# Step sizes as plain fp32 products of 64 columns, packed first loads, and gate weights stored in two pieces

## The chip, the cores and the metric

The kernel runs on one core of one Trainium2 chip. The metric is device time in microseconds (us). The kernel before takes 1026.54 us, the median of three runs (1025.41 to 1026.98). One more execution was taken by the hardware profiler: 1022.72 us, of which the span from the first to the last instruction is 1020.9 us. Every reading of the trace below is of that execution.

The core has a matmul engine (PE, with its weight loads listed apart as PEld), a vector engine (DVE), a scalar engine (ACT), a general engine (POOL) and the queue that issues most transfers (SP). Each takes its own instructions in order; they meet through semaphores.

## The reference

The program computes two decoder layers over one sequence of 256 tokens of width 2048: a Mamba-2 layer (layer A), then sliding-window attention (layer B). What this change touches, cut from the reference:

```python
# layer A
zxbcdt = x @ w_in                       # z 4096, xs 4096, B 1024, C 1024, dt 64 columns
dt = softplus(dt_raw + dt_bias)         # 256 x 64: the step sizes, one for each head
a  = -exp(a_log)
da_cum = cumsum(dt * a)                 # within a chunk of 128
decay  = exp(segsum(dt * a))            # scales every head's C B^T
# layer B
proj = x @ w_in                         # [q 2048 | gate 2048]
o = attention(q, k, v) * silu(gate)
```

All 64 step sizes are needed before any head's decay can be formed, and so before the first group of heads can finish.

## The kernel before

A product of full precision is made of three matmuls of the type fp32r (helper `mac`): each operand is split in a high part (ACT copies it to fp32r) and a low part (DVE subtracts that copy from the raw value), and high times high, high times low and low times high are summed in PSUM. The operand that is loaded into the array is a tile of weights (`wh`, `wl`), the one that streams is 256 tokens of x (`xH`, `xL`) or, in layer B, of the first layer's output (`x1H`, `x1L`).

Weights come in units of 128 columns by 2048 rows, 1 MB each, in the order of the list `srcs`. A unit is fetched by two transfers on SP into raw tiles (`wr`, five buffers), split on ACT and DVE (`load_unit`, L106 to L120), and multiplied in 16 tiles of 128 rows times three matmuls, 48 in all (`gemm_ws`, L273). `next_unit` (L170) keeps two units ahead of the one in use. Layer A has eight groups of ten units; group 0 begins with its four z units, then B, C and four xs units. The program's order inside each engine is fixed when the program is built, by a scheduler with costs and priorities of its own.

The start is special (`load_first`, L122, and L537): the first two units are the one of the step sizes (`wdt`, whose 64 columns are laid down twice to fill 128) and the first z unit. They are fetched beside x in six pieces of two to four tiles, and their matmuls alternate by pieces. The block of the step sizes then goes to `make_dt` (L290): ACT adds the bias, a chain of some twenty small operations on DVE makes the softplus and the running sums, the result goes to HBM (`rscr`, L318), and `load_decay` (L357) fetches rows of it, copied to all partitions, into `rb`. `sum_decay` (L369) makes the exponents of four heads from it, `cb` (L415) and `ymm` (L447) use them. The chain's DVE operations stand between the splits of the next units.

Where x stands in memory matters to the matmuls' pace. The class `Split` (L218) puts the first two tiles of `xH` and `xL` at bytes 0 and 64 modulo 256 and the rest at 192, while layer A's weights begin at 0. In layer B, `x1H` and `x1L` begin at 0. The 16 gate units of layer B (`gate_block`, L761: four blocks for each of j = 0 to 3) are shifted as a whole by 16 elements, 64 bytes (`split_tiles(16)`, L99 and L181), and so have their weights at 64.

Two more places of the program are named below: `ymm` multiplies plain fp32 tiles of 64 columns, two at a time, which write to rows 0 to 63 and 64 to 127 of one PSUM tile (L459); `cb` multiplies plain fp32 tiles of 128 columns (L419, L420).

Of the kernel before, what the change touches and what calls it, by code (L numbers as in the profile page):

```python
# [15 lines left out]
P = 128  # L16
S = 256
# [40 lines left out]
def trunk(ctx: ExitStack, tc: tile.TileContext, A: dict, out: bass.AP, dbg=None):  # L58
# [17 lines left out]
    def nm(s):  # L76
        uid[0] += 1
        return f"{s}_{uid[0]}"
# [15 lines left out]
    nc.gpsimd.memset(eps_t[:], EPS)  # L94

    class Unit:
        __slots__ = ("h", "l")

    def split_tiles(at):  # L99

        return [
            wp.tile([P, 2112], F32R, tag=tag, name=nm(tag), bufs=n)[:, at : at + 2048]
            for tag, n in (("wh", NH), ("wl", NL))
        ]

    def load_unit(src, at=0):  # L106
        u = Unit()
        hi, lo = split_tiles(at)
        raws = []
        for c in range(2):  # L110
            raw = wp.tile([P, 1024], F32, tag="wr", name=nm("wr"), bufs=NR)
            nc.sync.dma_start(raw[:], src[:, c * 1024 : (c + 1) * 1024])
            raws.append(raw)
        for c in range(2):
            sl = slice(c * 1024, (c + 1) * 1024)
            nc.scalar.activation(hi[:, sl], raws[c][:], AF.Copy)  # L116
            nc.vector.tensor_tensor(lo[:, sl], raws[c][:], hi[:, sl].bitcast(F32), ALU.subtract)  # L117
        u.h = hi
        u.l = lo
        return u  # L120

    def load_first(ss):  # L122

        us = [Unit() for _ in ss]
        for u in us:
            u.h, u.l = split_tiles(0)
        xraws = [
            ap.tile([P, 6, S], F32, tag="e", name=nm("xraw"), bufs=2),
            ap.tile([P, 6, S], F32, tag="e", name=nm("xraw"), bufs=2),
            ap.tile([P, 4, S], F32, tag="yz", name=nm("xraw"), bufs=1),  # L130
        ]
        for k0, k1 in FIRST:
            n = k1 - k0
            sl = slice(k0 * P, k1 * P)
            xraw = xraws[k0 // 6][:, k0 % 6 : k0 % 6 + n, :]
            for i, u in enumerate(us):
                raw = wp.tile([P, 1024], F32, tag="wr", name=nm("wr"), bufs=NR)[:, : n * P]
                nc.sync.dma_start(raw, ss[i][:, sl])
                if i == 0:
                    nc.sync.dma_start(xraw, A["xt"][:, k0:k1, :])  # L140
                nc.scalar.activation(u.h[:, sl], raw, AF.Copy)
                nc.vector.tensor_tensor(u.l[:, sl], raw, u.h[:, sl].bitcast(F32), ALU.subtract)
                if i == 0:
                    nc.scalar.activation(xH(k0, k1), xraw, AF.Copy)  # L144
                    nc.vector.tensor_tensor(xL(k0, k1), xraw, xH(k0, k1).bitcast(F32), ALU.subtract)  # L145
        return us


    srcs = [A["wdt"]]

    def wo_srcs(name, j):
        return [A[name][j * 4 + i] for i in range(4)]
# [9 lines left out]
    shifted = set()  # L162
    for what, j in B_ORDER:
        if what == "g":
            shifted.update(range(len(srcs), len(srcs) + 4))
        srcs += wo_srcs({"q": "wq", "g": "wg", "o": "wb"}[what], j)
    units = []
    used = [0]

    def next_unit():  # L170
        if not units:
            units.extend(load_first(srcs[:NFIRST]))
            nc.sync.dma_start(pc[:], A["pc"])
        while len(units) < min(used[0] + 1 + AHEAD, len(srcs)):
            if len(units) == 5:
                nc.sync.dma_start(cc[:], A["cc"])
            if len(units) in (8, 9):
                i = len(units) - 8
                nc.sync.dma_start(xr[:, i, :], A["xk"][:, i, :])
                nc.scalar.activation(xr[:, i, :], xr[:, i, :], AF.Copy, scale=ALPHA)  # L180
            units.append(load_unit(srcs[len(units)], 16 if len(units) in shifted else 0))  # L181
        used[0] += 1
        return units[used[0] - 1]

# [85 lines left out]
            stats(1, nb)  # L270
        done(1)

    def gemm_ws(us):  # L273
        pss = [mm_tile() for _ in us]
        for k0, k1 in FIRST:
            for ps, u in zip(pss, us):
                for k in range(k0, k1):
                    ks = slice(k * P, (k + 1) * P)
                    mac(
                        ps[:, :S], u.h[:, ks], u.l[:, ks], xH(k, k + 1)[:, 0, :], xL(k, k + 1)[:, 0, :],  # L280
                        k == 0, k == KT - 1,
                    )
        return pss


# [4 lines left out]
    def make_dt(ps):  # L290
        f = [ap.tile([P, S], F32, tag="sm", name=nm("f"), bufs=NSM) for _ in range(7)]
        u, e, rec, z, w, q, dt = [x[:] for x in f]
        nc.scalar.activation(u, ps[:, :S], AF.Identity, bias=pc[:, PC_DTB : PC_DTB + 1])
# [210 lines left out]

    def group(g):
        for b in range(10):
            if g == 0 and b < NFIRST - 1:
                ps = first_ps[b + 1]
            else:
                ps = gemm_ws([next_unit()])[0]  # L510
            k = BLOCKS0[b] if g == 0 else BLOCKS[b]
            if k >= 6:
                in_z(g, k - 6, ps)
            elif k >= 2:
                in_xs(g, k - 2, ps)
            else:
                (in_b, in_c)[k](g, ps)
            for fn, *a in plan.pop(10 * g + b, ()):
                fn(*a)
            if b in OUT_AT[g]:  # L520
                out_units(g - 1, [OUT_AT[g].index(b)])
        if g == NG - 1:
            out_units(g - 1, [1])
            out_units(g - 1, [2, 3])
            for t in sorted(plan):
                for fn, *a in plan[t]:
                    fn(*a)
        elif g > 0:
            out_units(g - 1, range(len(OUT_AT[g]), 4))
# [4 lines left out]
            for h in range(2):  # L534
                out_unit(*gs[g].y, h, u, nb, False, gs[g].rms)

    first_ps = gemm_ws([next_unit() for _ in range(NFIRST)])  # L537

    for c0, c1 in ((PC_CONV, PC_CONV + 240), (PC_NW, PC_NW + 32)):
        nc.vector.tensor_scalar(pc[:, c0:c1], pc[:, c0:c1], 0.5, None, ALU.mult)  # L540

    with tc.high_priority():
        dts = make_dt(first_ps[0])
        load_decay(0, 0)


    cs = cst.tile([P, 2, 8], F32, tag="cs", name="cs")
# [213 lines left out]
    def gate_block(j):  # L761
        t = bp.tile([P, 4, S], F32, tag="sg", name=nm("sg"), bufs=2)
        sg[j] = t
        for p_ in range(4):
            u = next_unit()
            ps = mm_tile()
            for k in range(KT):
                ks = slice(k * P, (k + 1) * P)
# [154 lines left out]
def _layout(inputs):  # L923
# [29 lines left out]
    a["wdt"] = wstat(np.concatenate([w[:, o_dt:], w[:, o_dt:]], 1))[0]  # L953
    conv = np.concatenate([f["a_conv_w"][0], f["a_conv_b"]], 0)
    corder = []
    for g in range(NG):
# [53 lines left out]
```

## Time and profile before

| | |
|---|---|
| median of three runs | 1026.54 us |
| profiled execution | 1022.72 us |
| its span, first to last instruction | 1020.9 us |
| PE busy | 1004.8 us, 98% of the span |
| DVE, ACT, POOL busy | 804.4, 519.5, 84.9 us |
| granted PE clock, mean | 0.999 of full speed |
| bytes read from HBM | 200.13 MB |

PE is busy nearly everywhere, and so a stage is worth reading at two places: where PE stands idle or works slowly (the start, single waits, the end), and at the step from the start of one matmul to the start of the next. The listed duration of a matmul (280 ns) is longer than that step, because matmuls overlap in the array. A plain fp32 matmul shows as two records in the trace. A row of the timeline has the start and the duration in us, the engine, the line of the kernel, the operation, the tiles (output, then inputs), the shapes and the count; a bracket has the idle time before it and what ended it.

### The profile page before, as it was taken

The numbers are of one execution on the slowest core, as the hardware profiler recorded it, in microseconds if no ns is written. First come the engines' busy times: TensorE is split into PE (matmuls) and PEld (weight loads), VectorE is DVE, ScalarE is ACT, GpSimd is POOL, SyncE is SP. The second block draws the span as 40 slices with busy tenths as digits, with TensorE's granted clock in tenths as the row PEclk, the third lists the DMA queues.
The fourth block names the chain that finished last, engine by engine and source line by source line (L and its number), as shares of the span: only waits on it lengthen the run. The fifth ranks groups of instructions, "written<-read, shape, count | busy, mean of one in ns | idle before, by whom it ended". The sixth has DMA issues, their size and how long they took to land. (4 is left out here: it accounts for less than half of the span.)

```text
span 1020.9 us, 17595 instructions
## 1 busy us (share of the span) xinstructions
PE 1004.8 (98%) x7028; PEld 908.3 (89%) x7028; DVE 804.4 (79%) x1212; ACT 519.5 (51%) x773; POOL 84.9 (8%) x112
## 2 busy tenths in 40 slices
PE   7999999999999999999999999999999999999997
PEld 6999989999999998999999999878988879879975
DVE  5989998977886895996896896897567785785776
ACT  6665654643743563563564464545445453453642
POOL 0000303003003002000200301301000000000002
PEclk9999999999999999999999999999999999999999
DMA  8896575674763865766566466646545445545532
GB/s 287 312 317 223 180 274 184 218 243 144 247 217 126 277 209 165 244 204 213 189 200 233 143 210 224 248 142 234 182 165 175 159 142 176 170 140 183 174 117 82
DMA packets 57170, 203.50 MB, mean 199 GB/s; under 512 B 6448, under 2 KB 8000, under 8 KB 56320
## 3 DMA queue, kind: packets, MB, share of 16 engines
q1 hardware_dynamic: 55728, 196.33, 57.5%
q0 software_dynamic: 1072, 5.53, 1.5%
q8 instruction: 55, 0.90, 0.3%
q10 hardware_dynamic: 288, 0.52, 0.1%
q14 instruction: 27, 0.22, 0.1%
HBM read 200.13 MB, written 2.23 MB: 198 GB/s over the span
## 5 line engine op out<-in xcount | busy, mean ns | idle before, releaser
L117 DVE TENSOR_TENSOR wl<-wr,wh 128x1024 fp32r<-128x1024 f32 x326 | 391.0, 1219 | 102.6 <-ACT wh L116 100.9
L116 ACT ACTIVATE wh<-wr 128x1024 fp32r<-128x1024 f32 x326 | 336.5, 1052 | 230.6 <-PE mm L187 71.3
L186 PE MATMUL mm<-xH,wh 128*128 128x256 f32 x1296 | 362.2, 280 | 7.5 <-ACT xH L144 5.8
L187 PE MATMUL mm<-xL,wh 128*128 128x256 f32 x1296 | 360.5, 278 | 0.1
L188 PE MATMUL mm<-xH,wl 128*128 128x256 f32 x1296 | 360.1, 278 | 0.4 <-DVE wl L117 0.4
L186 PEld LDWEIGHTS mm<-xH,wh 128*128 128x128 f32 x1296 | 244.5, 189 | 9.8 <-ACT xH L144 6.0
L187 PEld LDWEIGHTS mm<-xL,wh 128*128 128x128 f32 x1296 | 245.0, 189 | 1.3 <-DVE xL L145 0.3
L188 PEld LDWEIGHTS mm<-xH,wl 128*128 128x128 f32 x1296 | 245.0, 189 | 0.8 <-DVE wl L117 0.6
L246 PE MATMUL mm<-wh,yH 128*128 128x512 f32 x256 | 101.5, 396 | 0.0
L247 PE MATMUL mm<-wh,yL 128*128 128x512 f32 x256 | 99.9, 390 | 0.0
L248 PE MATMUL mm<-wl,yH 128*128 128x512 f32 x256 | 99.7, 389 | 0.0
L473 POOL TENSOR_TENSOR yz<-yz,z 128x256 f32<-128x256 f32 x32 | 29.8, 932 | 532.4 <-DVE yz L466 469.3
L186 PE MATMUL mm<-x1H,wh 128*128 128x256 f32 x256 | 72.5, 283 | 0.0
L188 PE MATMUL mm<-x1H,wl 128*128 128x256 f32 x256 | 71.6, 280 | 0.0
L187 PE MATMUL mm<-x1L,wh 128*128 128x256 f32 x256 | 71.6, 280 | 0.0
L347 DVE SCALAR_TENSOR_TENSOR cv<-mm,pc,cv 128x255 f32<-128x255 f32 x144 | 68.6, 476 | 3.6 <-ACT cv L345 2.7
L695 PE MATMUL mm<-wh,x1H 128*128 128x512 f32 x160 | 63.3, 396 | 0.0
L697 PE MATMUL mm<-wl,x1H 128*128 128x512 f32 x160 | 62.7, 392 | 0.2 <-DVE wl L117 0.2
L696 PE MATMUL mm<-wh,x1L 128*128 128x512 f32 x160 | 62.6, 391 | 0.2 <-DVE x1L L659 0.2
L246 PEld LDWEIGHTS mm<-wh,yH 128*128 128x128 f32 x256 | 48.1, 188 | 10.6 <-DVE z L412 0.9
L248 PEld LDWEIGHTS mm<-wl,yH 128*128 128x128 f32 x256 | 48.1, 188 | 10.2
L247 PEld LDWEIGHTS mm<-wh,yL 128*128 128x128 f32 x256 | 48.1, 188 | 8.9
(181 smaller groups left out, 1308.1 us busy)
## 6 DMA issues: line engine op xcount, KB each, us to landing
wr<-in_wa SPq DMA_DIRECT2D x158, 512.0 KB, 5.2
wr<-in_wo SPq DMA_DIRECT2D x64, 512.0 KB, 5.2
rb<-rscr SPq DMA_DIRECT2D x32, 512.0 KB, 4.6
wr<-in_wq SPq DMA_DIRECT2D x32, 512.0 KB, 4.2
wr<-in_wg SPq DMA_DIRECT2D x32, 512.0 KB, 5.2
wr<-in_wb SPq DMA_DIRECT2D x32, 512.0 KB, 4.3
wr<-in_wkv SPq DMA_DIRECT2D x8, 512.0 KB, 5.4
xr<-in_xk SPq DMA_DIRECT2D x2, 1024.0 KB, 9.5
```

Of the source, the lines that this page charges most:

```text
L116: nc.scalar.activation(hi[:, sl], raws[c][:], AF.Copy)
L117: nc.vector.tensor_tensor(lo[:, sl], raws[c][:], hi[:, sl].bitcast(F32), ALU.subtract)
L186: nc.tensor.matmul(ps, ah, bh, start=first, stop=False)
L187: nc.tensor.matmul(ps, ah, bl, start=False, stop=False)
L188: nc.tensor.matmul(ps, al, bh, start=False, stop=last)
L246: nc.tensor.matmul(ps[:], aH[:, k, hs], u.h[:, ks], start=k == 0, stop=False)
L247: nc.tensor.matmul(ps[:], aL[:, k, hs], u.h[:, ks], start=False, stop=False)
L248: nc.tensor.matmul(ps[:], aH[:, k, hs], u.l[:, ks], start=False, stop=k == 3)
L347: nc.vector.scalar_tensor_tensor(a[:, sft:], ps[:, : S - sft], w(3 - sft), a[:, sft:], ALU.mult, ALU.add)
L695: nc.tensor.matmul(ps[:], x1H[:, kk, hs], u.h[:, ks], start=kk == 0, stop=False)
L696: nc.tensor.matmul(ps[:], x1L[:, kk, hs], u.h[:, ks], start=False, stop=False)
L697: nc.tensor.matmul(ps[:], x1H[:, kk, hs], u.l[:, ks], start=False, stop=kk == KT - 1)
```

## The change

The unit `wdt` is gone. A new array `first` packs, for each of the 16 row tiles, 256 tokens of x, the 128 columns of the first z unit and the 64 columns of the step sizes: 448 columns, 229 KB for each tile. It is fetched in eight pieces of one to three tiles (`FIRST`); between them stand the two halves of the second z unit. The step sizes are made of 16 plain fp32 matmuls of 64 columns on the raw tiles, with no split: even tiles write rows 0 to 63 of a PSUM tile, odd tiles rows 64 to 127, and `make_dt` adds the two halves (two copies on ACT, one sum with the bias on DVE) in place of one ACT operation. A table `ORDER` sets how the matmuls of the step sizes (0), the first z unit (1) and the second z unit (2) are written. The scaling of the constants in `pc` is written after `make_dt`.

In layer B the gate units are stored in two pieces (`BROKEN`): the high part's first two tiles at byte 0 modulo 256, the rest at 64; the low part's first two tiles at 192, the rest at 64. `split_half` then needs two operations on ACT and two on DVE for a unit's first half.

What stands on PE at the program's start, before (`mm_182` is the block of the step sizes, `mm_183` the first z block):

```order
L186 MATMUL mm_182<-xH,wh_88 128x256
L186 MATMUL mm_183<-xH,wh_90 128x256
L187 MATMUL mm_182<-xL,wh_88 128x256
L188 MATMUL mm_182<-xH,wl_89 128x256
L186 MATMUL mm_182<-xH,wh_88 128x256
L187 MATMUL mm_182<-xL,wh_88 128x256
L188 MATMUL mm_182<-xH,wl_89 128x256
```

and in the changed program (`mm_149` holds the step sizes, `mm_150` the first z block, `first_*` are the raw pieces):

```order
L314 MATMUL mm_149<-first_92 64x256
L314 MATMUL mm_149<-first_98 64x256
L207 MATMUL mm_150<-xH,wh_88 128x256
L314 MATMUL mm_149<-first_104 64x256
L208 MATMUL mm_150<-xL,wh_88 128x256
L209 MATMUL mm_150<-xH,wl_89 128x256
L207 MATMUL mm_150<-xH,wh_88 128x256
L208 MATMUL mm_150<-xL,wh_88 128x256
L209 MATMUL mm_150<-xH,wl_89 128x256
L314 MATMUL mm_149<-first_104 64x256
L207 MATMUL mm_150<-xH,wh_88 128x256
L314 MATMUL mm_149<-first_110 64x256
```

The scheduler has set most of the plain matmuls singly between those of the z blocks. Of the 16, nine stand alone this way or wait for their own piece (tiles 0 to 8), tiles 9 to 13 stand in one run, and 14 and 15 in another, 30 matmuls of the z blocks before the end of the start.

On DVE, after the last splits of the start, before (`f_*` are the tiles of the step-size chain, `z_*` the z blocks; `wl_163`, `wl_173` the low parts of the second and third z units):

```order
L117 TENSOR_TENSOR wl_163<-wr_164,wh_162 128x1024
L117 TENSOR_TENSOR wl_163<-wr_166,wh_162 128x1024
L412 SCALAR_TENSOR_TENSOR z_321<-z_321,mm_183 128x256
L299 TENSOR_SCALAR f_284<-f_283 128x256
L117 TENSOR_TENSOR wl_173<-wr_174,wh_172 128x1024
L300 RECIPROCAL f_284<-f_284 128x256
```

and in the changed program (`wl_91` and `wl_308` are the low parts of the second and third z units):

```order
L136 TENSOR_TENSOR wl_91<-wr_144,wh_90 128x1024
L334 TENSOR_SCALAR aneg<-aneg 128x1
L329 SCALAR_TENSOR_TENSOR f_264<-mm_149,pc,f_265 128x256
L136 TENSOR_TENSOR wl_308<-wr_309,wh_307 128x1024
L448 SCALAR_TENSOR_TENSOR z_317<-z_317,mm_150 128x256
L136 TENSOR_TENSOR wl_308<-wr_311,wh_307 128x1024
L448 SCALAR_TENSOR_TENSOR z_330<-z_330,mm_151 128x256
L335 TENSOR_SCALAR f_266<-f_265 128x256
```

The sum that opens the chain now stands on DVE itself, ahead of the third z unit's splits, and everything behind it on DVE waits for the plain matmuls. From the sum to the chain's last operation there are ten splits of 128x1024 where there were twelve, one more z operation and one convolution operation of the B block. On PE nothing else is moved: from the third z block to the end the order is the same.

The diff, without the parts that only pass arguments on:

```diff
-NFIRST = 2
-FIRST = [(0, 2), (2, 4), (4, 6), (6, 9), (9, 12), (12, 16)]
+FIRST = [(0, 1), (1, 2), (2, 4), (4, 6), (6, 8), "h0", (8, 11), (11, 14), (14, 16), "h1"]
+ORDER = [(0, 0, 1), (1, 0, 2), (0, 1, 4), (1, 2, 6), (0, 4, 8), (1, 6, 8), (2, 0, 8), (0, 8, 14), (1, 8, 14),
+         (0, 14, 16), (1, 14, 16), (2, 8, 16)]
+FW = 256 + 128 + 64
...
+    WHOLE = [(0, 0, KT)]
+    BROKEN = [[(0, 0, 2), (272, 2, KT)], [(1840, 0, 2), (16, 2, KT)]]
+
+    def new_unit(places):
+        u = Unit()
+        u.parts = []
+        for tag, n, pl in (("wh", NH, places[0]), ("wl", NL, places[1])):
+            t = wp.tile([P, 2112], F32R, tag=tag, name=nm(tag), bufs=n)
+            u.parts.append([(t[:, o : o + (k1 - k0) * P], k0, k1) for o, k0, k1 in pl])
+        u.h, u.l = u.parts[0][0][0], u.parts[1][0][0]
+        return u
...
+    def split_half(u, raw, c):
+        for (h, k0, k1), (l, _, _) in zip(*u.parts):
+            a, b = max(k0, 8 * c), min(k1, 8 * c + 8)
+            if a < b:
+                sl = slice((a - k0) * P, (b - k0) * P)
+                v = raw[:, (a - 8 * c) * P : (b - 8 * c) * P]
+                nc.scalar.activation(h[:, sl], v, AF.Copy)
+                nc.vector.tensor_tensor(l[:, sl], v, h[:, sl].bitcast(F32), ALU.subtract)
...
+    def load_first():
+        us = [new_unit([WHOLE, WHOLE]) for _ in range(2)]
+        raws = {}
+        for piece in FIRST:
+            if isinstance(piece, str):
+                c = int(piece[1])
+                split_half(us[1], load_half(us[1], A["wa"][1], c), c)
+                continue
+            k0, k1 = piece
+            n = k1 - k0
...
+            raw = raw[:, : n * FW].rearrange("p (k c) -> p k c", c=FW)
+            nc.sync.dma_start(raw, A["first"][:, k0:k1, :])
+            h, l = [p[:, k0 * P : k1 * P].rearrange("p (k c) -> p k c", c=P) for p in (us[0].h, us[0].l)]
+            for dh, dl, v in ((xH(k0, k1), xL(k0, k1), raw[:, :, :S]), (h, l, raw[:, :, S : S + P])):
+                nc.scalar.activation(dh, v, AF.Copy)
+                nc.vector.tensor_tensor(dl, v, dh.bitcast(F32), ALU.subtract)
+            for k in range(k0, k1):
+                raws[k] = raw[:, k - k0, :]
+        return us, raws
...
+    def first_products():
+        us, raws = load_first()
+        units.extend(us)
+        nc.sync.dma_start(pc[:], A["pc"])
+        pss = [mm_tile() for _ in range(3)]
+        for i, k0, k1 in ORDER:
+            if i:
+                narrow(pss[i], us[i - 1], k0, k1)
+                continue
+            for k in range(k0, k1):
+                r = 64 * (k % 2)
+                nc.tensor.matmul(
+                    pss[0][r : r + 64, :S], raws[k][:, S + P :], raws[k][:, :S], start=k < 2, stop=k >= KT - 2
+                )
+        return pss
...
-        nc.scalar.activation(u, ps[:, :S], AF.Identity, bias=pc[:, PC_DTB : PC_DTB + 1])
+        for r in (0, 64):
+            nc.scalar.copy(e[r : r + 64], ps[64 - r : 128 - r, :S])
+        nc.vector.scalar_tensor_tensor(u, ps[:, :S], pc[:, PC_DTB : PC_DTB + 1], e, ALU.add, ALU.add)
...
-                mac(ps[:, :S], u.h[:, ks], u.l[:, ks], x1H[:, k, :], x1L[:, k, :], k == 0, k == KT - 1)
+                mac(ps[:, :S], u.tile(0, k), u.tile(1, k), x1H[:, k, :], x1L[:, k, :], k == 0, k == KT - 1)
```

More of the change, by code (lines that the diff above doesn't have):

```diff
@@ new lines, in load_unit @@
+    def load_unit(src, places):
+        u = new_unit(places)
+        raws = [load_half(u, src, c) for c in range(2)]
+        for c in range(2):
+            split_half(u, raws[c], c)
+        return u
+    def load_first():
[7 more added lines that the diff above has]
+            k0, k1 = piece
+            n = k1 - k0
+            if k0 == 14:
+                raw = ap.tile([P, 2 * 4 * S], F32, tag="rb", name=nm("first"), bufs=1)
+            elif n < 3:
+                raw = wp.tile([P, 1024], F32, tag="wr", name=nm("first"), bufs=NR)
+            else:
+                raw = ap.tile([P, 1536], F32, tag="e", name=nm("first"), bufs=2)
+            raw = raw[:, : n * FW].rearrange("p (k c) -> p k c", c=FW)
[7 more added lines that the diff above has]
+        return us, raws
@@ L535, in out_units @@
                 out_unit(*gs[g].y, h, u, nb, False, gs[g].rms)
-    first_ps = gemm_ws([next_unit() for _ in range(NFIRST)])
-    for c0, c1 in ((PC_CONV, PC_CONV + 240), (PC_NW, PC_NW + 32)):
-        nc.vector.tensor_scalar(pc[:, c0:c1], pc[:, c0:c1], 0.5, None, ALU.mult)
+    first_ps = first_products()
     with tc.high_priority():
```

96 lines of the change are left out of this document (31 added, 65 removed).

## The prediction

> **What bounds the kernel.** I read the page's busy line, then busy time by stretches, then the timeline of the first 30 us.
>
> ```profile
> PE 1004.8 (98%) x7028; PEld 908.3 (89%) x7028; DVE 804.4 (79%) x1212; ACT 519.5 (51%) x773; POOL 84.9 (8%) x112
> 0.00:10.00 10.00, 4.61 (x20) 4.31 (x21) 3.33 (x7) 4.92 (x9) 0.31 (x5) 1.00 0.74 224
> 14.00:20.00 6.00, 4.80 (x36) 4.20 (x35) 4.08 (x7) 2.94 (x6) 0.00 (x0) 1.00 0.93 301
> 26.00:40.00 14.00, 14.00 (x124) 14.00 (x123) 13.89 (x23) 8.90 (x10) 0.11 (x1) 1.00 0.84 289
> 40.00:100.00 60.00, 60.00 (x527) 58.66 (x526) 53.34 (x90) 35.65 (x46) 0.20 (x1) 1.00 0.82 284
> 1000.00:1021.00 21.00, 14.56 (x56) 9.82 (x54) 14.89 (x22) 5.28 (x11) 5.77 (x4) 0.94 0.27 100
> ```
>
> A stretch's row has its length, the busy time of PE, PEld, DVE, ACT and POOL, the granted clock, the DMA share and GB/s. PE idles in the first 20 us and the last 20, hardly between. But from 26 to 40 us DVE is busy 13.89 of 14: a second engine is full there.
>
> ```profile
> 3.35 0.42 ACT L141 ACTIVATE wh<-wr 128x256 fp32r<-128x256 f32 x1 [1.33 <-DMA wr<-in_wdt]
> 4.37 0.63 ACT L144 ACTIVATE xH<-xraw 128x512 fp32r<-128x512 f32 x1 [0.60 <-DMA xraw<-in_xt]
> 5.05 0.58 PE L186 MATMUL mm<-xH,wh 128*128 128x256 f32 x1 [5.05 <-ACT xH L144]
> 11.05 0.41 PE L186 MATMUL mm<-xH,wh 128*128 128x256 f32 x1
> 11.26 0.41 PE L187 MATMUL mm<-xL,wh 128*128 128x256 f32 x1
> 11.68 0.28 PE L186 MATMUL mm<-xH,wh 128*128 128x256 f32 x1
> 18.06 0.38 PE L186 MATMUL mm<-xH,wh 128*128 128x256 f32 x1 [0.70 <-ACT xH L144]
> 18.80 0.38 PE L186 MATMUL mm<-xH,wh 128*128 128x256 f32 x1 [0.35 <-ACT wh L141]
> 21.42 0.46 ACT L293 ACTIVATE f<-mm,pc 128x256 f32<-128x256 f32 x1
> 22.83 0.39 PE L188 MATMUL mm<-xH,wl 128*128 128x256 f32 x1 [0.42 <-DVE wl L117]
> 28.19 0.28 PE L186 MATMUL mm<-xH,wh 128*128 128x256 f32 x1
> 165.01 0.28 PE L186 MATMUL mm<-xH,wh 128*128 128x256 f32 x1
> 170.51 0.28 PE L186 MATMUL mm<-xH,wh 128*128 128x256 f32 x1
> ```
>
> The first matmul starts at 5.05, after a transfer and a split. Until 11.5 the step from matmul to matmul is 0.21 us; from 11.68 PE is at full speed, where a block of 48 takes 5.50 us (165.01 to 170.51), 0.115 a matmul. Then PE waits for data (18.06, 18.80, 22.83). At 28.19 three blocks are done (step sizes, first and second z) and the fourth starts. I measure the start by this point.
>
> **The start on PE.** Removed: one block, 5.5 us. Added: 16 plain products of 64 columns. Their price:
>
> ```profile
> 67.53 0.28 PE L188 MATMUL mm<-xH,wl 128*128 128x256 f32 x1
> 67.65 0.59 PE L419 MATMUL ax<-ct,bt 128*128 128x256 f32 x2
> 68.08 0.38 PE L420 MATMUL ax<-ct,bt 128*128 128x128 f32 x2
> 68.42 0.28 PE L187 MATMUL mm<-xL,wh 128*128 128x256 f32 x1
> 96.52 0.28 PE L188 MATMUL mm<-xH,wl 128*128 128x256 f32 x1
> 96.73 2.82 PE L459 MATMUL ax<-e,xd 128*64 128x256 f32 x32
> 99.48 0.39 PE L186 MATMUL mm<-xH,wh 128*128 128x256 f32 x1
> 99.82 0.28 PE L188 MATMUL mm<-xH,wl 128*128 128x256 f32 x1
> ```
>
> A plain product with 256 tokens takes 0.43 us (67.65 to 68.08), one with 128 half of that; this pair between fp32r matmuls costs 0.89 from 67.53 to 68.42, of which 0.23 are the fp32r steps: nothing is lost at its edges. The run at 96.73 is 16 products of 64 columns in pairs that share a slot: four slots of 0.43 and four of 0.215, 2.6 us. From 96.52 to 99.82 are 3.30, less three fp32r steps (0.35) 2.95. So 0.35 is lost, in the run or by going into 64-column tiles and back. Bounds for one such change of width: 0 (all of it lies inside the run) and 0.35 (all at the edges). The steps at the edges are the long ones (0.21 into the run, 0.34 for two matmuls after it), so I take 0.33.
>
> The Trainium skill, TensorEngine Tiling (Array Packing), section Tiling Modes, says that a change of tiling mode drains the engine; the 0.35 agrees, and by that rule every single plain product pays it.
>
> By the order shown there are 13 slots (tiles 0 to 8 one each, 9 to 13 three, 14 and 15 one): 13 x 0.43 = 5.6 us. Ten stretches of 64 columns, the first with no way in: 9.5 x 0.33 = 3.1. Two z blocks at 5.5: 11.0. In all 19.7 us at full speed, against 16.5 before. PE starts earlier: no split is needed, and the first piece (229 KB) lands between the row at 3.35 (131 KB landed) and the one at 4.37 (the next 262 KB too); I take 3.6. Slow clock: before, the fast pace came 6.4 us after the first matmul. I let it come after the same time, less 0.2, at 9.8, with bounds 7.5 and 12.5. Of the 6.2 us until then some 0.7 wait for pieces, and 5.5 at the slow pace (0.115/0.213) do 2.9 us of work; 16.8 are left, so the fourth block starts at 26.6 (24.6 to 28.3), against 28.19. Transfers keep up: h1 is the last of 4.72 MB, which at 301 GB/s from 2 us on lands at 17.7, and its matmuls come after 23. So PE is 1.6 us ahead; its old waits are gone, and most of that went into changes of width.
>
> **What takes the lead back.** The step sizes come later in the program's first part: the last plain products are followed by 30 matmuls of the z blocks, so they end at 26.6 - 3.5 = 23.1, where ACT read them at 21.42 before.
>
> ```profile
> 46.18 0.33 SPq L318 DMA_DIRECT2D rscr<-f  x1
> 57.25 0.48 DVE L375 SCALAR_TENSOR_TENSOR e<-rb,rtk 128x256 f32<-128x256 f32 x1 [0.92 <-DMA rb<-rscr]
> 66.71 0.48 DVE L375 SCALAR_TENSOR_TENSOR e<-rb,rtk 128x256 f32<-128x256 f32 x1 [0.22 <-DMA rb<-rscr]
> 78.03 2.35 DVE L117 TENSOR_TENSOR wl<-wr,wh 128x1024 fp32r<-128x1024 f32 x2
> 79.52 0.28 PE L188 MATMUL mm<-xH,wl 128*128 128x256 f32 x1
> ```
>
> The chain's result leaves at 46.18; its copy lands at 57.25, where DVE waits for it; DVE stays full, waits for the second copy at 66.71, and makes a weight split at 78.03 whose first half ends at 79.2. PE needs it at 79.52: 0.3 us of slack. So at this place the chain, not PE, decides how much of a lead survives.
>
> After: two ACT copies (0.42 each by the first row above) and the sum (0.48) bring DVE to 24.4. From 21.55 before to the send were 24.6 us; two splits fewer (2 x 1.18), a z and a convolution operation more (2 x 0.45), less some 0.6 of old waits: 22.5. The send is at 46.9, 0.7 late. A silu step of C (0.42) has moved ahead of the wait for the copy: 0.3 late at 78.03. Less the slack, PE stands within 0.1 of where it stood. The queue SP waits for the send too, and the units behind it arrive as much later; PE takes the first of them only in the 60s, so they cost nothing while the shift stays under some 3 us. The net gain of the start is 0.1 us, not 1.6; each us that the step sizes come earlier or later moves it by one, with the ends at 1.9 gained and 2.0 lost (fourth block at 24.8 or 28.6).
>
> **Gate units.**
>
> ```profile
> 724.39 0.28 PE L186 MATMUL mm<-x1H,wh 128*128 128x256 f32 x1
> 729.92 0.28 PE L188 MATMUL mm<-x1H,wl 128*128 128x256 f32 x1
> 798.30 0.28 PE L186 MATMUL mm<-x1H,wh 128*128 128x256 f32 x1
> 803.63 0.28 PE L188 MATMUL mm<-x1H,wl 128*128 128x256 f32 x1
> 778.00:783.00 5.00, 5.00 (x47) 1.00 0.76 257
> 875.50:880.50 5.00, 5.00 (x45) 1.00 0.30 110
> 954.80:959.80 5.00, 5.00 (x47) 1.00 0.00 2
> ```
>
> The first pair of rows are the first and last of one gate block's 48 matmuls, 47 steps of 0.1177; the second pair, another block, 47 of 0.1134. The pace holds for a whole block. Stretches of 5 us inside each of the 16 blocks hold 44 or 45 matmuls in eleven (875.50 is one) and 46 or 47 in five: the four of j = 1 and the last. Layer A's blocks, with their first two tiles at other offsets, all run at 0.1147 whatever precedes them. The new layout gives each stream of x1 against the next weight load the offsets that layer A has. If the pace follows: eleven blocks gain 48 x 0.0030 = 0.14 us, 1.6 in all; five lose 48 x 0.0013 = 0.06, 0.3 in all. Net 1.3 gained. Bounds: 0.3 lost (only the cost arrives) and 2.3 gained (all at 0.1134). The extra ACT and DVE operations (one each for 16 units, about 0.2 us) lie beside matmuls; PE there waits for neither. Were that cover gone they would cost 3 us each, spread over 240.
>
> **Sum.** 0.1 + 1.3 = 1.4 us gained: the profiled execution would go from 1022.72 to 1021.3. The three runs' median stands 3.8 us above that execution, so I forecast 1026.54 - 1.4 = 1025.1.
>
> **Rivals.** Under 0.2% (2.05 us) counts as the same, about what a measurement of this kernel tells from none.
>
> *The step sizes are early enough* (0.27). If full speed comes at 8 instead of 9.8, or a change of width costs 0.15, the fourth block starts at 25.2 and the send at 45.5: 1.5 gained, with the gates 2.8, 1023.7. For it: PE is dense from 3.6 on, where before it had gaps until 6. Against: the edges at 96.5 and 99.5. The skill's page TensorE: Matmul & The Clock Gate, Part 1, lets the clock open after one busy window of 3.4 us that runs freely, which would be 7.0 to 10.4 here; the trace's 6.4 us is within one or two such windows.
>
> *The gates do not follow* (0.15). The pace may hang on what precedes rather than on offsets; then 1026.5 with the start's 0.1.
>
> *Slower* (0.12). If the fast pace comes after 13, since single half-width products with pauses may keep the clock down, the fourth block starts after 28.7, the send after 49, and PE waits over 2 us at the split of 79: with gates unchanged 1029. It decides from 2 us of delay of the send, 3.4 if the gates gain.
>
> **Chances.** The forecast's case has 0.46: 0.13 of it faster by over 0.2%, the rest the same; the first rival 0.24 faster, 0.03 the same; the second the same; the slow one 0.10 slower, 0.02 the same. So 0.37 faster, 0.53 the same, 0.10 slower. The range, 1022.4 to 1028.0, reaches from the first rival with another 1.3 us to most of the slow one; the forecast's own case spans 1023.9 to 1026.3.
>
> **What would show it.** First plain matmul at 3.6; about 0.75 us for each that stands alone at full speed; fourth block near 26.6; the send near 46.9; a wait for a split at the block of 79 us, of about 1.5 us; all sixteen gate blocks at 0.1147. I am wrong if PE keeps its lead past 80 us, if the send is before 45, or if gate blocks keep 0.1177.

## The result and the profile after

The changed kernel took 1025.97 us against 1025.55 us before (medians of 12 runs each); one slow run of before, 3567.14 us, is left out of the ratio, and without it before's median is 1025.41. The ratio is 1.0006 with a 95% interval of 0.9996 to 1.0015. Measured a second time it was 1.0017 (1.0007 to 1.0028). So it is the same within 0.2%, with a lean to slower, where the forecast was 1.4 us of gain. Two changes of a few us cancel: the gate units gain somewhat more than expected, and the start, thought to be neutral, loses about as much.

The profiled execution took 1024.87 us (span 1023.1), 1.1 below its median; that of before, 1022.72, lies 2.8 below its own. Positions below are given against that favourable profile, and times against the medians.

The busy line of the page, and the timeline of PE at the start, the fourth block, around 79 us, and at the first and last matmuls of two gate blocks:

```profile
PE 1006.0 (98%) x7012; PEld 904.1 (88%) x7012; DVE 804.4 (79%) x1227; ACT 518.8 (51%) x788; POOL 84.8 (8%) x112
```

```profile
3.37 1.66 PE L314 MATMUL mm<-first 128*64 128x256 f32 x4 [3.37 <-DMA first<-in_first]
14.55 0.28 PE L209 MATMUL mm<-xH,wl 128*128 128x256 f32 x1
14.76 0.65 PE L314 MATMUL mm<-first 128*64 128x256 f32 x2
15.34 0.38 PE L207 MATMUL mm<-xH,wh 128*128 128x256 f32 x1
15.56 0.28 PE L208 MATMUL mm<-xL,wh 128*128 128x256 f32 x1
27.58 0.28 PE L207 MATMUL mm<-xH,wh 128*128 128x256 f32 x1
78.79 0.28 PE L208 MATMUL mm<-xL,wh 128*128 128x256 f32 x1
82.15 0.39 PE L209 MATMUL mm<-xH,wl 128*128 128x256 f32 x1 [3.08 <-DVE wl L136]
728.33 0.28 PE L207 MATMUL mm<-x1H,wh 128*128 128x256 f32 x1
733.68 0.28 PE L209 MATMUL mm<-x1H,wl 128*128 128x256 f32 x1
956.47 0.39 PE L207 MATMUL mm<-x1H,wh 128*128 128x256 f32 x1
962.11 0.28 PE L209 MATMUL mm<-x1H,wl 128*128 128x256 f32 x1
```

The fourth block starts at 27.58, 0.6 us before the 28.19 of before. At 82.15 PE has waited 3.08 us for a weight split. The first gate block then starts at 728.33, against 724.39: 3.9 us late. The last matmul of the last block starts at 962.11, against 959.89 before: 2.2 late, so the gate region gained 1.7.

Busy time by stretches (same columns as ahead of the prediction) around that wait, and inside the first and the last gate block:

```profile
78.00:82.00 4.00, 1.07 (x10) 0.86 (x8) 4.00 (x5) 2.33 (x4) 0.00 (x0) 1.00 0.02 8
82.00:87.00 5.00, 4.85 (x28) 4.85 (x29) 5.00 (x9) 1.22 (x2) 0.00 (x0) 0.66 0.61 201
87.00:92.00 5.00, 5.00 (x46) 5.00 (x45) 3.45 (x6) 2.75 (x4) 0.00 (x0) 1.00 0.89 281
729.00:734.00 5.00, 5.00 (x46) 5.00 (x45) 3.44 (x10) 1.52 (x3) 0.54 (x1) 1.00 0.62 188
957.00:962.00 5.00, 5.00 (x45) 5.00 (x44) 4.40 (x8) 2.63 (x6) 0.00 (x0) 1.00 0.01 3
```

After the wait the granted clock is 0.66 over 5 us, which costs another 1.7 us (5 x 0.34): 28 matmuls run where 46 would. With the wait this makes 4.8. In the gates 15 of the 16 blocks step at 0.1138 to 0.1141 us a matmul (728.33 to 733.68 are 47 steps of 0.1138), and only the last at 0.1178 (45 against 46 in 5 us); before, that last one was fast (0.1134), as were the four of j = 1, and eleven others ran at 0.1178. Eleven blocks that gain 47 x 0.0039 us, less the last one's loss of 0.2 and 0.1 of the four, make the 1.7. The expectations below put the new pace at 0.1133; it is about 0.1139.

Where the wait at 82.15 comes from is read from the bottom up in the timeline of SP, ACT and DVE ("x3" and "x5" are loads one after another):

```profile
51.15 1.72 SPq L126 DMA_DIRECT2D wr<-in_wa  x3
61.07 0.80 SPq L397 DMA_DIRECT2D rb<-rscr  x2
61.97 5.64 SPq L126 DMA_DIRECT2D wr<-in_wa  x5
73.31 1.06 ACT L135 ACTIVATE wh<-wr 128x1024 fp32r<-128x1024 f32 x1 [1.00 <-DMA wr<-in_wa]
74.28 1.48 ACT L424 ACTIVATE e<-e 128x1536 f32<-128x1536 f32 x1
75.66 0.40 ACT L386 ACTIVATE xs<-cv 128x256 f32<-128x256 f32 x1
76.08 0.43 DVE L387 SCALAR_TENSOR_TENSOR xs<-xs,cv 128x256 f32<-128x256 f32 x1 [2.59 <-ACT xs L386]
80.88 1.22 DVE L136 TENSOR_TENSOR wl<-wr,wh 128x1024 fp32r<-128x1024 f32 x1
```

The split at 80.88 stands on DVE behind the decays, these behind a silu step for which DVE waited 2.59 us; the silu stood on ACT behind the exp, and the exp behind a weight copy that waited for its load until 73.31. On SP three loads go out between the first and the second copy of the decays (rb) and five behind the second. In the timeline of the kernel before it was four and four:

```profile
49.86 4.17 SPq L112 DMA_DIRECT2D wr<-in_wa  x4
60.34 0.80 SPq L361 DMA_DIRECT2D rb<-rscr  x2
61.57 4.91 SPq L112 DMA_DIRECT2D wr<-in_wa  x4
70.28 1.06 ACT L116 ACTIVATE wh<-wr 128x1024 fp32r<-128x1024 f32 x1 [1.28 <-DMA wr<-in_wa]
```

One load (the 20th half unit of weights, sent at 53.70 before and at 61.97 here) had moved behind a trigger that waits until DVE has used up the first copy. ACT misses the second load behind it: that one was sent only 0.7 us later than before (63.86 against 63.16), right behind the moved one, and ACT could copy it 3.0 us later (73.31 against 70.28).

And further back, the timeline of SP, ACT and DVE of the changed kernel at the start, with two stretches of it:

```profile
19.40 8.22 SPq L126 DMA_DIRECT2D wr<-in_wa  x2
24.18 0.74 ACT L328 COPY f<-mm 64x256 f32<-64x256 f32 x2 [6.01 <-PE mm L314]
24.95 0.48 DVE L329 SCALAR_TENSOR_TENSOR f<-mm,pc,f 128x256 f32<-128x256 f32 x1 [5.52 <-ACT f L328]
```

```profile
19.00:22.00 3.00, 3.00 (x24) 2.19 (x23) 0.44 (x2) 0.00 (x0) 0.00 (x0) 1.00 1.02 414
24.00:27.00 3.00, 3.00 (x27) 2.94 (x26) 1.44 (x2) 2.79 (x6) 0.00 (x0) 1.00 0.04 10
```

The copies of the step sizes, which need the last plain product, stand on ACT and DVE ahead of weight copies whose data is there. Both engines stand still for 5.5 to 6 us, no load buffer comes free, and SP sends nothing from 19.40 until the second load of its row, at 27.3; from 24 to 27 the transfers carry 10 GB/s. Before, loads went out at 20.0, 22.8 and 24.6.

### The profile page after: what moved, and what is told of

Its sections match the earlier page's. It is cut to its first block, busy times and chain, and to the rows that moved or that the text cites. A ratio compares the mean times of both kernels' runs of the same rounds, so it can differ in the third digit from the quotient of the medians.

```text
span 1023.1 us, 17562 instructions
## 1 busy us (share of the span) xinstructions
PE 1006.0 (98%) x7012; PEld 904.1 (88%) x7012; DVE 804.4 (79%) x1227; ACT 518.8 (51%) x788; POOL 84.8 (8%) x112
## 5 line engine op out<-in xcount | busy, mean ns | idle before, releaser
L136 DVE TENSOR_TENSOR wl<-wr,wh 128x1024 fp32r<-128x1024 f32 (+2 forms) x342 | 393.8, 1170 | 100.2 <-ACT wh L135 99.0
L135 ACT ACTIVATE wh<-wr 128x1024 fp32r<-128x1024 f32 (+2 forms) x342 | 337.4, 1012 | 229.7 <-PE mm L208 65.5
L207 PE MATMUL mm<-xH,wh 128*128 128x256 f32 x1280 | 357.9, 280 | 1.0 <-DVE cv L383 1.0
L209 PE MATMUL mm<-xH,wl 128*128 128x256 f32 x1280 | 355.7, 278 | 3.1 <-DVE wl L136 3.1
L208 PE MATMUL mm<-xL,wh 128*128 128x256 f32 x1280 | 356.1, 278 | 0.0
L207 PEld LDWEIGHTS mm<-xH,wh 128*128 128x128 f32 x1280 | 241.3, 189 | 5.0 <-ACT wh L166 1.5
L209 PEld LDWEIGHTS mm<-xH,wl 128*128 128x128 f32 x1280 | 241.8, 189 | 4.4 <-DVE wl L136 3.3
L208 PEld LDWEIGHTS mm<-xL,wh 128*128 128x128 f32 x1280 | 241.7, 189 | 2.1 <-issue 1.1
```

Of the source, the lines that this page charges most:

```text
L135: nc.scalar.activation(h[:, sl], v, AF.Copy)
L136: nc.vector.tensor_tensor(l[:, sl], v, h[:, sl].bitcast(F32), ALU.subtract)
L207: nc.tensor.matmul(ps, ah, bh, start=first, stop=False)
L208: nc.tensor.matmul(ps, ah, bl, start=False, stop=False)
L209: nc.tensor.matmul(ps, al, bh, start=False, stop=last)
```

## Experiments

Ratios are to the kernel before, measured beside the run. After the experiments a table has the positions of all profiles.

**The two parts apart.** The start alone (gates stored as before), and the gates alone (the kernel before with the new storage). The edit of the first, in the changed kernel:

```diff
-    BROKEN = [[(0, 0, 2), (272, 2, KT)], [(1840, 0, 2), (16, 2, KT)]]
+    BROKEN = [[(16, 0, KT)], [(16, 0, KT)]]
```

> The changed kernel with layer B's gate weights whole and shifted by 16 columns again, as before. Theory of the gates (the pace of a gate block follows where its weights are stored): in the changed kernel 15 of 16 blocks run at 0.1133 us a matmul, before 5 did and 11 at 0.1178; with the old places some eleven blocks go back to 0.118, and this kernel is 1.7 us slower than the changed one, about 1027.6, with the same wait of PE near 79 us. Rival (the pace follows what runs ahead of a block or when it comes): it stays at 0.113 in most blocks, and the time at 1026.

> The kernel before with the gate weights in two pieces, its start untouched. Theory of the gates: 15 of 16 blocks at 0.1133, 1.7 us faster than before, ratio 0.9983. Rival (pace by what runs ahead): eleven blocks stay at 0.118, ratio 1.000.

Start alone: 1.0016 (1.0004 to 1.0028), 1.6 us slower than before; gates alone: 0.9974 (0.9964 to 0.9983), 2.7 us faster. The gate blocks of `start_only` step as before (eleven at 0.1178), those of `gates_only` as in the changed kernel (fifteen at about 0.1139), so the pace goes with the storage. In the trace of `gates_only` the gate region gains 1.8 us; the measured 2.7 has an interval from 1.7. Added up, the two parts give a ratio of 0.999; the whole measured 1.0006 and 1.0017. The intervals leave room for the first, hardly for the second, so it isn't shown that the two parts simply add.

**What about the storage?** Each of the four groups of gate blocks with another one:

```diff
+    S16 = [(16, 0, KT)]
+    LAYOUT = [[WHOLE, WHOLE], BROKEN, [BROKEN[0], S16], [S16, BROKEN[1]]]
-            broken.update(range(len(srcs), len(srcs) + 4))
+            broken.update((i, LAYOUT[j]) for i in range(len(srcs), len(srcs) + 4))
```

> The changed kernel with another place of the gate weights for each of the four groups of gate blocks: group 0 both parts whole and unshifted, group 1 both in two pieces (as in the changed kernel), group 2 the high part in two pieces and the low part whole, shifted by 16 columns, group 3 the high part whole, shifted, and the low part in two pieces. Before, groups 0, 2 and the first three blocks of group 3 ran at 0.1178. Theory (the pace follows the offset between each moving stream of x1 and the weights loaded beside it, for either part): groups 2 and 3 run between 0.1133 and 0.1178, one part right and one wrong. Rival (any place but the one before is good): all groups at 0.1133 to 0.1147.

Stretches inside a block of group 0, one of group 1, two of group 2 and two of group 3:

```profile
727.00:732.00 5.00, 5.00 (x44) 5.00 (x43) 3.66 (x9) 1.50 (x2) 0.54 (x1) 1.00 0.66 191
780.50:785.50 5.00, 5.00 (x46) 5.00 (x45) 4.38 (x12) 0.73 (x2) 0.00 (x0) 1.00 0.67 235
859.00:864.00 5.00, 5.00 (x45) 5.00 (x44) 3.79 (x10) 1.87 (x3) 0.00 (x0) 1.00 0.44 156
866.00:871.00 5.00, 5.00 (x46) 4.87 (x46) 2.44 (x3) 1.89 (x5) 0.00 (x0) 1.00 0.56 161
936.00:941.00 5.00, 5.00 (x46) 5.00 (x46) 3.62 (x10) 1.71 (x3) 0.00 (x0) 1.00 0.50 179
949.00:954.00 5.00, 5.00 (x45) 5.00 (x44) 4.93 (x9) 0.86 (x2) 0.00 (x0) 1.00 0.35 112
```

Whole and unshifted the blocks step at 0.1199, slower than with the old shift (0.1178); with one part in pieces, two blocks of four step at 0.1133 to 0.1140 and two at 0.1178. (This kernel was run once, for its profile, so its time is not compared.) So both parts count, and something that changes from block to block within a group too; which it is stays open.

**The same kernel again,** with no edit.

> The changed kernel as it is, for a second profile and more times. Theory (the start differs from execution to execution, since the clock opens at different times, from 10 to 14 us in the profiles so far, and PE's wait near 79 us goes from 0.6 to 3.4): the fourth block starts between 26.5 and 29.5, PE waits 0.5 to 3.5 us near 79, and where it waits over 2 us it runs some 4 us at the slow clock after it; ratio 1.000 to 1.002. Rival (the wait of 3.4 and the slow clock are in every execution): the same 3.3 and 4 us again, within 0.3.

The ratio was 1.0017. The fourth block started at 29.49, the clock had opened at 16.5 instead of 10.7, and at 83.10 PE had waited 2.11 us, with no slow clock after it. `start_only` and `layouts`, whose programs are the same up to the gates, waited 0.47 and 1.76 us there. The wait is thus in every profile of this start, in sizes from 0.5 to 3.1 us; the slow clock after it is not.

**The load back in its place on SP.**

```diff
+        if held and c == 1 and len(units) == 10:
+            for d in held:
+                tc.add_manual_dep(
+                    d.ins, dma.ins.name,
+                    mybir.DependencyInfo(mybir.DependencyClass.NoSync, mybir.DependencyReason.DATA),
...
```

Here `held` has the two triggers of the second copy, which are issued behind that load without waiting for it to land.

> The changed kernel with one edit: the second broadcast of the decays (rb) is queued on SP behind the 20th half unit of weights, as in the kernel before, no longer ahead of it. Theory of the queue: in the changed kernel this one load comes some 8 us later, the two after it are pushed back 3 us, ACT's copy, the exp and the silu behind it and DVE's split follow, and PE waits 3.3 us at 78.9 and then runs 4 us at the slow clock (2 us lost). With the load back in its place the wait falls to under 0.8 us, the clock stays open, and the kernel gains 4 to 5 us: about 1021.5, ratio to the kernel before 0.996. Rival (the late step sizes, sent at 48.4 instead of 46.2, are the cause, whatever the queue): the send stays at 48.4, PE still waits 2 us or more near 79, and the time stays within 1.5 us of the changed kernel.

0.9977 (0.9965 to 0.9989): 2.4 us faster than before, about 3 to 4 faster than the changed kernel, a little short of the 0.996 expected. The timeline at the same place:

```profile
51.94 5.33 SPq L126 DMA_DIRECT2D wr<-in_wa  x4
71.44 1.05 ACT L143 ACTIVATE wh<-wr 128x1024 fp32r<-128x1024 f32 x1
73.40 0.42 DVE L396 SCALAR_TENSOR_TENSOR xs<-xs,cv 128x256 f32<-128x256 f32 x1
79.04 2.35 DVE L144 TENSOR_TENSOR wl<-wr,wh 128x1024 fp32r<-128x1024 f32 x2
80.53 0.28 PE L218 MATMUL mm<-xH,wl 128*128 128x256 f32 x1
```

The weight copy no longer waits for its load, nor DVE for the silu, nor PE for the split, although the send was later still (49.3) and the hole at the start was as long (loads at 19.0 and 28.9). The rival, that the late step sizes decide, falls. But the edit moved two more things in the scheduler's orders: a split came ahead of the sums of the second copy on DVE (68.38 against 71.42), and on ACT the silu came ahead of the exp (72.71 and 74.46; 75.66 and 74.28 in the changed kernel). So this run alone doesn't show that the load's place is the whole cause. `wide` below has the load ahead with the changed kernel's order of exp and silu on ACT, and there DVE waits 0.21 us for the silu, not 2.59; but its send was earlier too (47.12).

**The step sizes earlier, in two ways.** Once with plain products 128 columns wide, and once gathered:

```diff
-                    pss[0][r : r + 64, :S], raws[k][:, S + P :], raws[k][:, :S], start=k < 2, stop=k >= KT - 2
+                    pss[0][:, :S], raws[k][:, S + 64 : S + 64 + P], raws[k][:, :S],
+                    start=k == 0, stop=k == KT - 1,
```

> The changed kernel with the step sizes' plain products taken 128 columns wide (the last 64 of the z unit beside the 64 of the step sizes, from the same packed load), added up in one place instead of even and odd halves. Theory of the width: a product alone now costs 0.43 us and nothing at its edges, against 0.77; the sixteen take 6.9 us instead of 8.9, the step sizes are sent some 2 us earlier (46.5), the fourth block starts near 25.7, and SP's order has the load ahead of the second broadcast again: no wait over 0.8 us at 79, time 1019 to 1021.5. Rival (the 0.33 lies in the change between plain fp32 and fp32r, not in the width): a product alone still costs 0.76, the sixteen take 10 us, the fourth block starts at 28.7 and the send is later than 48.4.

```diff
+ORDER = [(1, 0, 6), (0, 0, 8), (1, 6, 8), (2, 0, 8), (1, 8, 14), (0, 8, 16), (1, 14, 16), (2, 8, 16)]
```

> The changed kernel with the plain products gathered: 6 stretches of 64 columns instead of 10, 10 slots instead of 13, and PE begins with products of the z block. Theory of the width (0.43 us a slot and 0.34 for each stretch): the plain products take 6.3 instead of 8.8 us, the sum of the step sizes comes 1.5 to 2.5 us earlier, and with it the send (near 46.5) and the split; ratio 0.998 to 0.9995. Theory of the clock (single half-width products with pauses between them keep the clock shut): it opens by 11.5, as in the three profiles with the old start (7.7, 9.4, 11.5), and not at 15.7 or 16.5 as in two of five with the new one. Rival (the step sizes' place does not matter): 1.001.

The timeline of PE in `wide` with one product alone:

```profile
14.71 0.59 PE L313 MATMUL mm<-first 128*128 128x256 f32 x2
14.95 0.47 PE L209 MATMUL mm<-xH,wl 128*128 128x256 f32 x1
15.26 0.28 PE L207 MATMUL mm<-xH,wh 128*128 128x256 f32 x1
```

At full width a product alone takes 14.71 to 15.26, less one fp32r step 0.43; at 64 columns it is 14.55 to 15.56 in the changed kernel, less two steps 0.77. The 0.34 lie in the change of width, and not in the change between plain fp32 and fp32r. `wide` started its fourth block at 26.2, and its scheduler put the load ahead again; PE waited 0.74 us, yet it took 1024.21 us, ratio 0.9993 (0.9980 to 1.0005), and not 1019 to 1021.5: the lead went later (below).

The timeline of `gather` from the send on, and the stretch behind the wait:

```profile
46.86 0.33 SPq L353 DMA_DIRECT2D rscr<-f  x1
51.00 0.80 SPq L396 DMA_DIRECT2D rb<-rscr  x2
59.67 0.48 DVE L410 SCALAR_TENSOR_TENSOR e<-rb,rtk 128x256 f32<-128x256 f32 x1 [2.33 <-DMA rb<-rscr]
83.25 0.58 PE L208 MATMUL mm<-xH,wl 128*128 128x256 f32 x1 [4.36 <-DVE wl L135]
```

```profile
83.00:88.00 5.00, 4.75 (x22) 4.75 (x23) 5.00 (x8) 1.01 (x2) 0.00 (x0) 0.50 0.56 177
```

It sent the step sizes at 46.86, 1.6 us earlier than the changed kernel, and gained nothing: 1.0017 (1.0007 to 1.0027). But the send took 3.7 us to land, against 1.8, so the copy went out at 51.00, later than the 50.26 of the changed kernel, and PE waited 4.36 us, with the load still behind the second copy. So a cheaper set of plain products and an earlier send gain nothing by themselves, against my theory; what step sizes that arrive earlier would gain, this run doesn't show. The clock opened at 13.1 there, not by 11.5, though PE began with products of z. One narrow product stood among them (9.10), and PE had been idle for 2.40 us until 8.16, so the narrow products are not cleared: without them it opened at 11.0 and 9.6 (`wide`, `wide_cb_late`), with them at 9.9 to 16.5 in nine profiles. Whether they are the cause is not shown.

**Easing DVE and ACT.** The masked products of the first group one block later (in the changed kernel, in `wide`, and in `gates_only`), and two half units of weights ahead of the step sizes:

```diff
-TD, TS, CB0 = 5, 5, 8
+TD, TS, CB0 = 5, 5, 9
```

> The changed kernel with one number changed: the masked products of the first group (cb, on DVE 4.0 us with its two multiplications of the decays) are taken up one block later, so that DVE makes the two splits that PE needs near 79 us ahead of them. The queue on SP stays as in the changed kernel. Theory of DVE's row (PE waits because the late load holds up ACT, and the split stands behind the decays on DVE): the split is 4 us earlier, the wait near 79 falls to 0, the clock stays open, and the kernel gains 2 to 4 us on the changed one: ratio 0.997 to 0.999. Rival (the load itself comes too late for PE): the wait stays over 1 us, ratio 1.000 or more.

> The wide plain products of the run before with the same number changed (cb one block later). There PE waited 0.9 us at 77.4, 1.1 at 131 and 0.85 at 282 with 1.5 us of slow clock after it. Theory (PE's lead of 2 us from the start is lost wherever the row of DVE has less slack than the lead): the wait at 77 goes, the one at 131 stays (about 1.3 of slack was there in the kernel before), so of the 2 us only some 1.3 are kept, and with the gates' 1.8 the ratio is 0.997. Rival (the lead is carried through): ratio 0.9955.

> The kernel before with the gate weights in two pieces (the run gates_only, ratio 0.9974) and cb one block later. Theory (typical executions of the kernel before lose some of their time at the split near 79 too, where the profile shows 0.27 us of slack and that of gates_only a wait of 0.45): a gain of 0.3 to 1 us on gates_only, ratio 0.9965 to 0.997. Rival (the start of the kernel before loses nothing there): ratio 0.9974 as before.

```diff
+    units.append(load_unit(srcs[2], [WHOLE, WHOLE]))
-            nc.scalar.copy(e[r : r + 64], ps[64 - r : 128 - r, :S])
+            sums[0] = tc.keep_in_program_order(nc.scalar.copy(e[r : r + 64], ps[64 - r : 128 - r, :S]))
...
+                for s in sums[2 * i : 2 * i + 2]:
+                    st.enter_context(tc.issue_after(s.ins))
```

> The changed kernel with the two half units of weights that come after the start copied and split ahead of the step sizes' copies, on ACT and on DVE (in the changed kernel they stand behind them: ACT waits 6.0 us for PE at 24.18, DVE 5.5 us at 24.95, and SP sends no load between 19.4 and 27.29 because no buffer comes free). Theory of the hole (the loss of the start comes from these 6 us in which the row of weights stands still): the load after 19.4 goes out near 21, DVE has two splits less to make between the sum and the send, the send comes near 46.5 instead of 48.4 to 49.9, PE waits under 1 us near 79, and the kernel gains 3 to 4 us on the changed one: ratio to before 0.9975. Rival (the row is not what limits; the late sum is): the send stays at 48 or later, the wait stays over 2 us, the ratio at 1.000 to 1.002.

> Both edits that ease DVE's row: the two half units ahead of the step sizes, and cb one block later. Theory of the hole: with the row of weights ahead, PE's lead of the start (0.6 to 1.5 us) is no longer given back between 84 and 140 us as in cb_late, so that some 1 us is gained on cb_late and on weights_first: ratio 0.9965 to 0.997. Rival (a lead of PE is given back downstream whatever the row does): 0.9975 to 0.9985, like cb_late.

`cb_late` came to 0.9985 (0.9973 to 0.9997), `weights_first` to 0.9982 (0.9971 to 0.9993), both 2 to 4 us faster than the changed kernel, and neither waits for the split of 79. `cb_late` kept the load behind the second copy, and DVE still waited for the silu there (1.73 us at 75.05), but the split no longer stood behind the decays: it takes the late load and that place together to make PE wait. `weights_first` sent its next load at 21.18, as expected; its send did not come earlier (49.24, the clock having opened at 14.7), and gained nevertheless. It also brought the load ahead of the second copy, so what the hole costs without that stays open. `weights_first_cb_late` reached 0.9975 (0.9965 to 0.9984), not below 0.997: the rival's value. `wide_cb_late` reached 0.9971 (0.9959 to 0.9983) and `gates_cb_late` 0.9969 (0.9957 to 0.9981), the fastest median ratio here, 0.3% below before. That one has the old start, and its step from the 0.9974 of `gates_only` is within the noise. No form of the new start with the new gates was measured clearly faster than `gates_only`: with the wait at 79 gone, the start costs about nothing, and a gain from it is not shown.

Where the leads went shows in the waits of `cb_late` further on:

```profile
133.25 0.50 PE L267 MATMUL mm<-wh,yH 128*128 128x512 f32 x1 [0.82 <-DVE xr L274]
284.12 0.36 PE L207 MATMUL mm<-xH,wh 128*128 128x256 f32 x1 [1.72 <-DVE cv L383]
```

DVE is the last to arrive again, at two later places. At the second, every profile waits about 1.0 us, that of before too (0.99 at 281.91), so only what is over that belongs to the start: 0.7 here, 0.8 in `wide`, 1.0 in `wide_cb_late`. The table has, for every profile, the end of the last slow step of the start, the start of the fourth block, PE's idle time at the split near 79 us, and the start of the first gate block against 724.39 (us):

| profile | start | clock opens | fourth block | idle at split | first gate block |
|---|---|---|---|---|---|
| before | old | 11.5 | 28.2 | - | 0 |
| gates_only | old | 7.7 | 28.4 | 0.30 | +2.0 |
| gates_cb_late | old | 9.4 | 28.0 | - | -0.5 |
| after | new | 10.7 | 27.6 | 3.08, then slow | +3.9 |
| again | new | 16.5 | 29.5 | 2.11 | +4.5 |
| start_only | new | 9.9 | 26.7 | 0.47 | -0.3 |
| layouts | new | 10.7 | 27.5 | 1.76 | +2.1 |
| gather | new, gathered | 13.1 | 27.4 | 4.36, then slow | +5.6 |
| queue_back | new | 15.7 | 29.2 | - | +1.4 |
| cb_late | new | 10.6 | 27.3 | - | +1.9 |
| wide | new, wide | 11.0 | 26.2 | 0.74 | +2.7 |
| wide_cb_late | new, wide | 9.6 | 25.9 | - | +2.0 |
| weights_first | new | 14.7 | 29.3 | - | +3.1 |
| weights_first_cb_late | new | 11.9 | 27.7 | - | +1.3 |

The last column hardly knows the fourth: leads of 2 us are gone by the gates, and the profile with the latest fourth block but two (`queue_back`) is among the better ones. With the new start (`after` and `gather` aside, the two with the longest waits at 79) PE waits 0.2 to 0.8 us for DVE at 131 to 137 us, where before does not wait. Why DVE comes late there, the runs don't show.

## Why the prediction was right or wrong

Right in its class (no change) and its range, but by luck, since two errors partly cancel: the gain of 1.4 us did not come, because the start, taken as 0.1 us gained, lost 1.6 (0.4 to 2.9), while the gates gained more than the 1.3 expected.

- *First plain matmul at 3.6*: 3.37. *About 0.75 us for a product alone*: 0.77, and the cause was right: `wide` shows the 0.34 go with the width. The Trainium skill, TensorEngine Tiling (Array Packing), section Tiling Modes, has a change of tiling mode drain the engine; the 0.34, and nothing at full width, agree.
- *Fourth block at 26.6, clock at 9.8*: 27.58 and 10.7, within the bounds. But the bounds of the clock, 7.5 to 12.5, were too narrow: `again`, `queue_back` and `weights_first` opened at 14.7 to 16.5.
- *The send at 46.9, 0.7 late, each us moving the start's gain by one*: 48.43; the sum began at 24.95 and not near 24.0. This rule is the step that failed: `gather` sent at 46.86 and gained nothing, as its copy went out no earlier; `queue_back` sent at 49.3, copied at 51.05, later than the changed kernel in both, and gained 3.
- *The units behind the send cost nothing while the shift stays under 3 us*: this was the missed term. I shifted SP's loads with the send and did not price the one that changes places with the second copy of the decays. Nor did I ask what waits behind the copies of the step sizes on ACT and DVE; the hole of 6 us stood in their orders.
- *A wait of about 1.5 us at the split of 79*: there, from 0.47 to 3.08 us in four profiles of this start. That a wait of 3 us also shuts the clock, for 1.7 us more, I had not priced.
- *Gate units gain 1.3*: 1.7 in the trace and 2.7 (1.7 to 3.7) by `gates_only`, the pace about 0.1139 rather than 0.1147, with the last block slowed. That the storage sets the pace was shown; that the new blocks would take over layer A's pace with its offsets was not borne out, and neither the slow last block nor the mixed blocks of `layouts` follow from it. The rival that the gates don't follow falls.
- *The rivals*: "slower, 1029" named the right place, but took the late clock and the late send as its condition; it happened in the profile of `after` with an early clock. "Early enough" was not met in full (fourth block at 25.2, send at 45.5): `wide` came nearest in one edit, with 26.2 and 47.12, and its 0.9993 is not faster than the gates alone. `wide_cb_late`, with 25.9, gained 3.0 us, about that rival's 2.8, but `gates_cb_late` gained as much with the old start.

## What to carry to other kernels

Where a change moves an instruction that waits (a copy of a result, a trigger for a reused buffer), list what stands behind it on its in-order engine and compare the queue's order row by row: one 512 KB load behind one waiting trigger came with a wait of 3 us at an engine three steps away. A lead on the busiest engine is worth only what the second busiest can follow; here DVE was full from 26 to 40 us and nearly so to 100, and PE waited for it at later places until the leads of the start were gone by the gates. And with executions of one kernel between 1020.91 and 1027.89 us, one profile is one draw: take a second before explaining a wait by its size.

## What the runs showed of the hardware

- A wait can cost twice. Idle times of 3.08 and 4.36 us on PE were followed by the slow pace (granted clock 0.66 and 0.50 over 5 us), and so was one of 1.84 in `wide` at 283 (0.66); waits of 2.11, 2.04 and 1.76 us (`again`, `wide_cb_late` at 284, `layouts`) were not. By these traces it matters where a wait falls. In their clock records the slow stretches begin at 82.74 (`after`), 284.04 (`wide`) and 81.33 (`gather`), last 3.41, 3.41 and 6.83 us, and lie 21, 80 and 20 times 3.413 us behind the point at which the clock had opened (11.06, 10.97 and 13.07 in the records; the table above has the end of the last slow step). In the 3.41 us ahead of each, PE was idle for 2.83, 1.85 and 2.44 us. With the time of all 14 profiles cut in such steps, no other step between 30 and 1000 us that began with the clock open has PE idle for more than 1.76 us, and the clock stayed open after each. The Trainium skill, TensorE: Matmul & The Clock Gate, Part 1, has the clock fall back after an idle window of about 3.4 us; here windows that were idle for little more than half did it, so the measurement decides. Its free-running window fits that like waits act differently. For the opening it fits only in part: one or two such windows are 3.4 to 6.8 us (an estimate from that page of the Trainium skill), and the clock opened anywhere from 3 to 13 us after the first matmul; what delayed the later ones is not shown.
- The pace of the same 128x256 fp32r matmul was 0.1133, 0.1139, 0.1147, 0.1178 or 0.1199 us, for whole blocks: up to 0.3 us of 5.4 in a block. In layer B it changed with where the weights lay (`gates_only`, `layouts`), though not with that alone: blocks with the same storage differ.
